# Splitting the rows of a triangular inverse over two copies, and moving copies of one recurrent branch from VectorE to ScalarE

## The chip, the cores and the metric

The kernel runs on one core of a Trainium2 chip. A core has TensorE (matrix products, into PSUM), VectorE (called DVE in the profile), ScalarE (ACT), GpSimd (POOL) and SyncE (SP, which here starts the weight loads). Each engine works through its own queue in order. The metric is the time of one execution on the device in microseconds; less is better.

## The reference

One transformer block, float32, 256 tokens of width 2048: half a SwiGLU feed-forward (hidden width 5632), a hybrid mixer, half a second feed-forward, each with a norm before and after. The mixer multiplies by `w_in`, sends 1024 columns each as r, k, v into a recurrent branch (16 heads of 64), 1024 into a pooling branch, and gates the two. The recurrent branch is, per head,

```python
def step(state, inp):
    r_t, w_t, k_t, v_t, a_t, b_t = inp
    sa = einsum('bhvk,bhk->bhv', state, a_t)
    state = state * w_t + sa[..., None] * b_t + v_t[..., None] * k_t
    y_t = einsum('bhvk,bhk->bhv', state, r_t)
```

with a = -kk and b = kk * a_h, where `kk` is k times `k_k`, normalised per head, and k itself is multiplied by `1 + (a - 1) * k_a`.

## The kernel before

Every large product is made of three float32r matmuls on a high and a low part of each operand (`mm3`, and the same three in `gemm_ch`). `load_w` brings a weight tile of 128 x 1024 in by SyncE's queue; ScalarE rounds it to wH (L101) and VectorE subtracts to get wL (L102). There are four buffers of the raw tile and five each of wH and wL. TensorE then runs 512-column matmuls (`gemm_tok`, L109 to L111) or 256-column ones (`gemm_ch`, L174 to L176).

The mixer runs in the order `a0 p a1 b0 b1 b2 b3`: recurrent branch for the first 512 channels, the four pooling windows (`pool_window`, L516 evacuates a product into zb; `pool_mix`, L547 and L548 write yb), the recurrent branch for the other 512, then the pooled projection. `rwkv` is the recurrent branch and is called twice ("half-branches" below). It turns the recurrence into chunks of 64 tokens:

- L584 to L649 work out the decay sums (lam, ilam by an exponential), kk (L609, normalised through pn and pk), k2 (L636, L638), and the per-head sums.
- L668 to L680 make a copy of v with neighbouring heads swapped, transpose it on TensorE (pV, L674) and copy it into EVs (ScalarE) and ODs (VectorE).
- L685 to L695 build the operands BK and AR. L706 multiplies them: eight PSUM tiles pA, each holding four chunks of one head's 64 x 64 products. ScalarE copies the first product into Xab (L710); VectorE masks the second into Xrb (L711) and the other half of the partitions back into AR (L713). pB transposes BK (L720, L724).
- The strictly triangular 64 x 64 matrix of each of the 16 (pair, chunk) groups per partition half must be inverted. Its two 32 x 32 diagonal blocks are inverted on VectorE. Four transposes (L733), one per 32 partitions, put the matrices on partitions: of each 32 partitions, 16 hold the 16 matrices and the other 16 hold a second copy of the same. Then 31 steps each make a product (L740, into pr) and add it (L742), over all rows found so far; both copies do the same work. Two transposes bring the inverse back (L746 to t11, L747 to td), L753 and L755 copy it into tt, and pM and pX (L761, L770) make the off-diagonal block.
- For each chunk, pU, pSa, pS and pY apply the inverse and carry the state; then a group norm and the output yH, yL.

All tiles of `rwkv` lie in fifteen registers `s.R[n]` of 128 x 1024 (in the profile they are all called R). PSUM has a pool of four tiles for the products above (mm, mc) and four for the small ones (pV, pA and so on). The program only states the work; the order of the instructions in each engine's queue is set when it is built, by a planner that simulates their costs, and weight conversions and most evacuations of `gemm_tok` and `gemm_ch` have raised priority.

Of the kernel before, what the change touches and what calls it, by code (L numbers as in the profile page):

```python
# [10 lines left out]
AF = mybir.ActivationFunctionType  # L11
ALU = mybir.AluOpType
AX = mybir.AxisListType
PSUM = bass.MemoryType.PSUM

P = 128
# [8 lines left out]
C = 64  # L25
# [19 lines left out]
class Block:  # L45
# [279 lines left out]
    def setup_mixer(s, prm):  # L325
        nc = s.nc
        s.col = {}

        def load_rows(rows, name):
            n = sum(r for _, r in rows)  # L330
            t = s.unit((P, 1024), F32, name)
            nc.gpsimd.memset(t[:, :P], 0.0)
            o = 0
            offs = []
            for nme, r in rows:
                offs.append((nme, o, r))
                if nme == "mu":
                    nc.sync.dma_start(out=t[o:o + 26, :P],
                                      in_=prm["mu"][:26 * P].rearrange("(k p) -> k p", p=P))
                    nc.sync.dma_start(out=t[o + 26:o + 27, :RCOLS - 26 * P],  # L340
                                      in_=prm["mu"][26 * P:].unsqueeze(0))
                    o += 27
                    continue
                nc.sync.dma_start(out=t[o:o + r, :P],
                                  in_=prm[nme].rearrange("(k p) -> k p", p=P))
                o += r
            ps = s.psum("pr")
            nc.tensor.transpose(ps[:, :P], t[:, :P], s.ident)
            ct = s.const([P, o], name)
            nc.vector.tensor_copy(ct, ps[:, :o])  # L350
            for nme, o, r in offs:
                s.col[nme] = ct[:, o:o + (27 if nme == "mu" else r)]

        load_rows(ROWS, "cols1")
        load_rows(ROWS2, "cols2")
        omu = s.const([P, 27], "omu")
        nc.vector.tensor_scalar(out=omu, in0=s.col["mu"], scalar1=-1.0, scalar2=1.0,
                                op0=ALU.mult, op1=ALU.add)
        s.col["omu"] = omu
        oka = s.const([P, 8], "oka")  # L360
        nc.vector.tensor_scalar(out=oka, in0=s.col["k_a"], scalar1=-1.0, scalar2=1.0,
                                op0=ALU.mult, op1=ALU.add)
        s.col["oka"] = oka
        m = s.mask = s.const([P, 2, C], "mask")
        nc.gpsimd.memset(m, 1.0)
        for h in range(2):
            for q, op in ((0, ALU.is_gt), (1, ALU.is_ge)):
                a = m[h * 64:h * 64 + 64, q]
                nc.gpsimd.affine_select(out=a, in_=a, compare_op=op, fill=0.0, base=0,
                                        pattern=[[1, C]], channel_multiplier=-1)  # L370
        s.bones = s.const([P, P], "bones")
        nc.gpsimd.memset(s.bones, 0.0)
        for h in range(2):
            nc.gpsimd.memset(s.bones[h * 64:h * 64 + 64, h * 64:h * 64 + 64], 1.0)
        s.zi = 0
        s.zb = [s.const([P, S + 16], f"zb{i}") for i in range(2)]
        for z in s.zb:
            nc.gpsimd.memset(z[:, :16], 0.0)
        s.rcp = s.const([P, 16], "rcp")
        for t in range(16):  # L380
            nc.gpsimd.memset(s.rcp[:, t:t + 1], 1.0 / (t + 1))
# [172 lines left out]
    def rwkv(s, hf, r, k, v, lz, prm, yH, yL):  # L554
        nc = s.nc
# [50 lines left out]
        kk = reg(3, 4, S)  # L606
        sq = reg(4, 4, S)
        for i in range(4):
            V.tensor_scalar(out=kk[:, i], in0=k[:, i], scalar1=col("k_k", i), scalar2=None,  # L609
                            op0=ALU.mult)  # L610
        A.activation(out=fl(sq), in_=fl(kk), func=AF.Square)
        ps = s.psum("pn")
        for i in range(4):
# [19 lines left out]

        k2 = reg(5, 4, S)
        for i in range(4):
            V.tensor_scalar(out=k2[:, i], in0=a[:, i], scalar1=col("k_a", i),  # L636
                            scalar2=col("oka", i), op0=ALU.mult, op1=ALU.add)
        V.tensor_tensor(out=fl(k2), in0=fl(k2), in1=fl(k), op=ALU.mult)  # L638


# [11 lines left out]
        BK = [reg(7, *t5), reg(8, *t5)]  # L652
        AR = [[reg(9, *t5), reg(10, *t5)], [reg(11, *t5), reg(12, *t5)]]
        EVs, ODs = reg(13, 4, NCH, C), reg(14, 4, NCH, C)
        Xab, Xrb = reg(4, 16, C), reg(5, 16, C)
        BKt = [reg(1, *t5), reg(2, *t5)]

        for q in range(2):
# [6 lines left out]
        vs = reg(10, 4, S)  # L665
        vp = lambda t: t.rearrange("p i (a b t) -> p (i a) b t", a=2, b=2)
        for b in range(2):
            V.tensor_copy(vp(vs)[:, :, b], vp(v)[:, :, 1 - b])  # L668
        for pr in range(2):
            pss = []  # L670
            for src in (v, vs):
                ps = s.psum("pV").rearrange("p (i c) -> p i c", i=4)
                for i in range(4):
                    T.transpose(ps[:, i], src[:, i, pr * P:pr * P + P], s.ident)  # L674
                pss.append(ps)
            for b in range(2):
                c = 2 * pr + b
                pe, po = pss[1 - b], pss[b]
                A.copy(EVs[O, :, c], pe[O, :, :64])
                V.tensor_copy(ODs[E, :, c], po[E, :, 64:])  # L680
        for q in range(2):
            i2 = slice(2 * q, 2 * q + 2)
            for h, R in ((0, E), (1, O)):
# [14 lines left out]
        for q in range(2):  # L698
            ar, bk = AR[q], BK[q]
            for i in range(2):  # L700
                g4 = slice(8 * q + 4 * i, 8 * q + 4 * i + 4)
                pAs = [s.psum("pA").rearrange("p (c j t) -> p c j t", c=NCH, j=2)
                       for _ in range(2)]
                for c in range(NCH):
                    for h, R in ((0, E), (1, O)):
                        T.matmul(pAs[h][:, c], bk[R, i, c], ar[h][R, i, c], start=True,  # L706
                                 stop=True)
                for h, R, RK in ((0, E, O), (1, O, E)):
                    ps = pAs[h]
                    A.copy(Xab[R, g4], ps[R, :, 0])  # L710
                    V.tensor_tensor(out=Xrb[R, g4], in0=ps[R, :, 1],  # L711
                                    in1=mb[R, :, 1].to_broadcast([64, NCH, C]), op=ALU.mult)
                    V.tensor_tensor(out=ar[h][RK, i], in0=ps[RK],  # L713
                                    in1=mb[RK].to_broadcast([64, NCH, 2, C]), op=ALU.mult)
            pBs = [s.psum("pB").rearrange("p (i c t) -> p i c t", i=2, c=NCH)
                   for _ in range(2)]
            for i in range(2):
                for c in range(NCH):
                    for h, R in ((0, E), (1, O)):
                        T.transpose(pBs[h][:, i, c],  # L720
                                    bk[R, i, c].rearrange("p j t -> p (j t)"),
                                    s.ident[R, R])
            for h in range(2):
                A.copy(BKt[q][:, :, :, h], pBs[h])  # L724
# [1 line left out]
        G.memset(ODs[O, :, 0], 0.0)  # L726


        wt, tw = reg(3, 32, 32), reg(0, 32, 32)
        for b in range(4):  # L730
            R = slice(b * 32, b * 32 + 32)
            o = (b % 2) * 32
            V.transpose(out=wt[R], in_=Xab[R, :, o:o + 32].rearrange("p g t -> p t g")  # L733
                        .unsqueeze(2).to_broadcast([32, 32, 2, 16]))
        G.memset(tw, 0.0)
        G.memset(s.R[0][:, 0:1024:33], 1.0)
        for kq in range(31):
            n, m = kq + 1, 31 - kq
            pr = s.rtmp("pr")[:, :n * m].rearrange("p (a b) -> p a b", a=n)
            V.tensor_tensor(out=pr, in0=wt[:, kq + 1:, kq].unsqueeze(1).to_broadcast([P, n, m]),  # L740
                            in1=tw[:, :n, kq:kq + 1].to_broadcast([P, n, m]), op=ALU.mult)
            V.tensor_tensor(out=tw[:, :n, kq + 1:], in0=tw[:, :n, kq + 1:], in1=pr,  # L742
                            op=ALU.add)
        tt, td, t11 = reg(7, 16, C), reg(8, 32, 32), reg(3, 32, 32)
        m1 = s.R[0][:, :512].rearrange("p (g t) -> p g t", g=16)
        V.transpose(out=t11, in_=tw)  # L746
        V.transpose(out=td, in_=tw.rearrange("p s t -> p t s"))  # L747
        for b in range(4):
            R = slice(b * 32, b * 32 + 32)
            o = (b % 2) * 32  # L750
            src = td[R, :, :16].rearrange("p t g -> p g t")
            if b < 2:
                A.copy(tt[R, :, o:o + 32], src)  # L753
            else:
                V.tensor_copy(tt[R, :, o:o + 32], src)  # L755
        for h in range(2):
            G.memset(tt[h * 64 + 32:h * 64 + 64, :, :32], 0.0)
        ps = s.psum("pM").rearrange("p (g t) -> p g t", g=16)
        for g in range(16):
            for h in range(2):  # L760
                T.matmul(ps[h * 64 + 32:h * 64 + 64, g],  # L761
                         Xab[h * 64:h * 64 + 32, g, 32:64],
                         t11[h * 64:h * 64 + 32, :, g], start=True, stop=True)
        A.copy(m1[32:64], ps[32:64])
        V.tensor_copy(m1[96:128], ps[96:128])
# [194 lines left out]
```

## Time and profile before

| | |
|---|---|
| median of 3 runs | 2156.44 us (2155.68 to 2157.66) |
| the profiled execution | 2156.19 us, its span 2154.4 us |
| TensorE busy | 2114.6 us, 98% of the span |
| VectorE busy | 1288.9 us, 60% |
| ScalarE busy | 1086.2 us, 50% |
| GpSimd busy | 78.2 us, 4% |
| mean granted TensorE clock | 0.992 |
| first half-branch, about | 856 to 1075 us |
| second half-branch, about | 1075 to 1280 us |

Busy time is the time in which an engine had an instruction in work. Matmuls overlap: a 512-column one is shown as 0.39 us long, but one starts every 0.226 us, so a busy TensorE may still run below its rate. A line such as "PE mc L174 <- DVE zb L516: 5.0, 1, 5.0" says that TensorE's matmul of line 174 waited 5.0 us in total, once, at most 5.0 us, for VectorE's write or read of zb in line 516. In the time order a row gives start, length, engine, line, operation, output and input with their shapes, and the count of instructions merged into it. The granted clock is TensorE's, as a share of full speed.

### The profile page before, as it was taken

How to read it: one execution, taken by the hardware profiler on the slowest of the kernel's cores; microseconds unless marked ns; L12 is line 12 of the kernel's file. 1: busy time of each engine (PE TensorE's matmuls, PEld its weight loads, DVE VectorE, ACT ScalarE, POOL GpSimd, SP SyncE). 2: the span in 40 equal slices, each digit the busy share in tenths (PEclk: the TensorE clock that was granted, in tenths of full speed). 3: DMA queues.
4: the chain of work that ended last, by engine and by line, in shares of the span. 5: the costliest groups of instructions: out<-in, count | busy, mean ns of one | idle time of the engine just before them, and what ended most of it. 6: DMA issues, size and time to landing. Idle time of an engine off the chain costs nothing.

```text
span 2154.4 us, 28711 instructions
## 1 busy us (share of the span) xinstructions
PE 2114.6 (98%) x11077; PEld 1774.9 (82%) x11077; DVE 1288.9 (60%) x1609; ACT 1086.2 (50%) x1516; POOL 78.2 (4%) x164
## 2 busy tenths in 40 slices
PE   8999999999999999889999999999999999999998
PEld 6888888888888799889788778878888888888886
DVE  5556555555444556997689656565556555654444
ACT  6565556555444554444454434455565556554442
POOL 1000000000000100101110110010000000000000
PEclk9999999999999999999999999999999999999999
DMA  7656666667666666255556666656667666676664
GB/s 234 195 177 207 195 195 186 198 205 242 195 195 192 194 173 182 84 157 164 147 153 179 178 223 193 192 179 202 194 177 213 193 191 184 206 252 192 193 193 136
DMA packets 223219, 406.06 MB, mean 188 GB/s; under 512 B 12991, under 2 KB 48969, under 8 KB 223081
## 3 DMA queue, kind: packets, MB, share of 16 engines
q1 hardware_dynamic: 216937, 383.11, 58.9%
q0 software_dynamic: 6144, 21.11, 2.7%
q8 instruction: 87, 1.43, 0.3%
q14 instruction: 51, 0.42, 0.1%
HBM read 395.78 MB, written 8.39 MB: 188 GB/s over the span
## 4 chain that ended last, share of the span: by engine, by line
PE 90%; DVE 6%; issue 2%; ACT 1%; DMA 1%; POOL 0%; DVEq 0%; POOLq 0%; SPq 0%; ACTq 0%
PE mm L111 27%; PE mm L110 27%; PE mm L109 27%; PE mc L174 2%; PE mc L175 2%; PE mc L176 2%; DVE wL L102 2%; DVE R L733 1%; DVE pr L740 1%; DMA w<-in_ffn_gate_dram 1%; ACT wH L101 0%; DVE R L742 0%; PE tr L206 0%; DVE R L713 0%; ACT junk L239 0%
## 5 line engine op out<-in xcount | busy, mean ns | idle before, releaser
L102 DVE TENSOR_TENSOR wL<-w,wH 128x1024 fp32r<-128x1024 f32 (+2 forms) x734 | 884.9, 1212 | 768.7 <-ACT wH L101 767.5
L101 ACT CAST wH<-w 128x1024 fp32r<-128x1024 f32 (+2 forms) x734 | 761.0, 1043 | 901.0 <-PE mm L111 708.8
L109 PE MATMUL mm<-wH,xH 128*128 128x512 f32 x2496 | 974.9, 391 | 6.7 <-ACT xH L212 6.7
L111 PE MATMUL mm<-wH,xL 128*128 128x512 f32 x2496 | 975.4, 391 | 5.2 <-DVE xL L213 5.2
L110 PE MATMUL mm<-wL,xH 128*128 128x512 f32 x2496 | 974.4, 391 | 0.5 <-DVE wL L102 0.4
L109 PEld LDWEIGHTS mm<-wH,xH 128*128 128x128 f32 x2496 | 470.3, 188 | 107.3 <-ACT xH L212 9.7
L111 PEld LDWEIGHTS mm<-wH,xL 128*128 128x128 f32 x2496 | 470.2, 188 | 104.4 <-DVE xL L213 6.8
L110 PEld LDWEIGHTS mm<-wL,xH 128*128 128x128 f32 x2496 | 470.2, 188 | 98.8 <-DVE wL L102 1.4
L174 PE MATMUL mc<-xH,wH 128*128 128x256 f32 (+1 forms) x560 | 160.3, 287 | 5.0 <-DVE zb L516 5.0
L175 PE MATMUL mc<-xH,wL 128*128 128x256 f32 x560 | 160.4, 287 | 0.0
L176 PE MATMUL mc<-xL,wH 128*128 128x256 f32 x560 | 159.5, 285 | 0.0
L232 ACT COPY x<-T 32x256 f32<-32x256 f32 x352 | 141.9, 403 | 3.9
L174 PEld LDWEIGHTS mc<-xH,wH 128*128 128x128 f32 (+1 forms) x560 | 107.0, 191 | 6.2 <-issue 5.4
L175 PEld LDWEIGHTS mc<-xH,wL 128*128 128x128 f32 x560 | 107.1, 191 | 0.6
L176 PEld LDWEIGHTS mc<-xL,wH 128*128 128x128 f32 x560 | 107.1, 191 | 0.4
L251 ACT ACTIVATE sg<-mm,rs 128x512 f32<-128x512 f32 x44 | 30.2, 690 | 21.3 <-PE mm L111 21.3
L252 DVE SCALAR_TENSOR_TENSOR sg<-mm,rs,sg 128x512 f32<-128x512 f32 x44 | 31.6, 751 | 13.2 <-ACT sg L251 13.2
L283 POOL DMA_DIRECT2D gb<-in_ln_ffn_post_dram x4 | 2.2, 562 | 926.7 <-DVE xL L236 893.5
L239 ACT ACTIVATE junk<-mm 128x512 bf16<-128x512 f32 x24 | 14.3, 595 | 34.5 <-PE mm L111 34.5
L286 DVE TENSOR_TENSOR fg<-mm,gb 128x512 f32<-128x512 f32 x24 | 16.5, 691 | 24.5 <-ACT junk L239 24.5
L257 DVE SCALAR_TENSOR_TENSOR sg<-mm,rs,sg 128x512 f32<-128x512 f32 x44 | 30.9, 744 | 0.0
L222 DVE STREAM_TRANSPOSE T<-sg 128x512 f32<-128x512 f32 x44 | 30.9, 702 | 0.0
(220 smaller groups left out, 1030.2 us busy)
## 6 DMA issues: line engine op xcount, KB each, us to landing
w<-in_ffn_up_dram SPq DMA_DIRECT2D x176, 512.0 KB
w<-in_ffn_down_dram SPq DMA_DIRECT2D x176, 512.0 KB
w<-in_ffn_gate_dram SPq DMA_DIRECT2D x174, 512.0 KB
w<-in_w_in_dram SPq DMA_DIRECT2D x128, 512.0 KB
w<-in_w_out_dram SPq DMA_DIRECT2D x32, 512.0 KB
w<-in_w_proj_b_dram SPq DMA_DIRECT2D x16, 512.0 KB
w<-in_w_proj_a_dram SPq DMA_DIRECT2D x16, 512.0 KB
hsp<-fg POOLq DMA_DIRECT2D x16, 256.0 KB, 5.1
```

The source lines that it names most:

```text
L101: nc.scalar.copy(vH, v)
L102: nc.vector.tensor_tensor(out=vL, in0=v, in1=vH.bitcast(F32), op=ALU.subtract)
L109: nc.tensor.matmul(ps, aH, bH, start=start, stop=False)
L110: nc.tensor.matmul(ps, aH, bL, start=False, stop=False)
L111: nc.tensor.matmul(ps, aL, bH, start=False, stop=stop)
L174: s.nc.tensor.matmul(o, h_, xH, start=k == 0, stop=False)
L175: s.nc.tensor.matmul(o, l_, xH, start=False, stop=False)
L176: s.nc.tensor.matmul(o, h_, xL, start=False, stop=k == KT - 1)
L222: s.nc.vector.transpose(out=T1[:, h * 512:h * 512 + 512], in_=src)
L232: nc.scalar.copy(dst[q * 32:q * 32 + 32, :, :, i], src[i * 32:i * 32 + 32, :, :, q])
L252: nc.vector.scalar_tensor_tensor(out=sg, in0=ps, scalar=rs[h], in1=sg, op0=ALU.mult, op1=ALU.mult)
L257: nc.vector.scalar_tensor_tensor(out=sig[h], in0=ps, scalar=rs[h], in1=sig[h], op0=ALU.mult, op1=ALU.mult)
```

## The change

In the recurrence, the two copies of each matrix now share the rows: copy d (0 or 1) holds rows d, d+2, d+4 and so on. So step kq covers kq // 2 + 1 rows instead of kq + 1, and tw is half as large. The ones on its diagonal are set by two ScalarE copies from a new constant `dup` (128 x 2, made once from the identity) in place of a GpSimd fill. The way back is two transposes of 128 x 512, the second reading the first's result, in place of two of 128 x 1024.

The diagonal blocks are no longer transposed out of Xab in four pieces. ScalarE copies them out of each pA tile in two pieces of 32 partitions into Xd, laid out with the 16 matrices adjacent, and the off-diagonal block in a third piece into Xo; Xd and Xo share the register that Xab had. One transpose of 128 x 1024, which reads Xd twice, makes wt.

Four kinds of VectorE instructions with one tensor input move to ScalarE: kk's product, k2's scale and bias, the swapped copy of v, and the ODs copies. So do the two copies into tt that VectorE made.

```diff
--- before.py
+++ after.py
@@ -368,6 +368,9 @@
                 a = m[h * 64:h * 64 + 64, q]
                 nc.gpsimd.affine_select(out=a, in_=a, compare_op=op, fill=0.0, base=0,
                                         pattern=[[1, C]], channel_multiplier=-1)
+        s.dup = s.const([P, 2], "dup")
+        nc.vector.tensor_reduce(out=s.dup, in_=s.ident.rearrange("p (b d g) -> p d b g", b=4, d=2),
+                                axis=AX.XY, op=ALU.add)
         s.bones = s.const([P, P], "bones")
         nc.gpsimd.memset(s.bones, 0.0)
         for h in range(2):
@@ -606,8 +609,7 @@
         kk = reg(3, 4, S)
         sq = reg(4, 4, S)
         for i in range(4):
-            V.tensor_scalar(out=kk[:, i], in0=k[:, i], scalar1=col("k_k", i), scalar2=None,
-                            op0=ALU.mult)
+            A.activation(out=kk[:, i], in_=k[:, i], func=AF.Copy, scale=col("k_k", i))
         A.activation(out=fl(sq), in_=fl(kk), func=AF.Square)
         ps = s.psum("pn")
         for i in range(4):
@@ -633,8 +635,8 @@
 
         k2 = reg(5, 4, S)
         for i in range(4):
-            V.tensor_scalar(out=k2[:, i], in0=a[:, i], scalar1=col("k_a", i),
-                            scalar2=col("oka", i), op0=ALU.mult, op1=ALU.add)
+            A.activation(out=k2[:, i], in_=a[:, i], func=AF.Identity, scale=col("k_a", i),
+                         bias=col("oka", i))
         V.tensor_tensor(out=fl(k2), in0=fl(k2), in1=fl(k), op=ALU.mult)
 
 
@@ -652,7 +654,9 @@
         BK = [reg(7, *t5), reg(8, *t5)]
         AR = [[reg(9, *t5), reg(10, *t5)], [reg(11, *t5), reg(12, *t5)]]
         EVs, ODs = reg(13, 4, NCH, C), reg(14, 4, NCH, C)
-        Xab, Xrb = reg(4, 16, C), reg(5, 16, C)
+        Xrb = reg(5, 16, C)
+        Xd = s.R[4][:, :512].rearrange("p (t g) -> p t g", g=16)
+        Xo = s.R[4][:, 512:].rearrange("p (g t) -> p g t", g=16)
         BKt = [reg(1, *t5), reg(2, *t5)]
 
         for q in range(2):
@@ -665,7 +669,7 @@
         vs = reg(10, 4, S)
         vp = lambda t: t.rearrange("p i (a b t) -> p (i a) b t", a=2, b=2)
         for b in range(2):
-            V.tensor_copy(vp(vs)[:, :, b], vp(v)[:, :, 1 - b])
+            A.copy(vp(vs)[:, :, b], vp(v)[:, :, 1 - b])
         for pr in range(2):
             pss = []
             for src in (v, vs):
@@ -677,7 +681,7 @@
                 c = 2 * pr + b
                 pe, po = pss[1 - b], pss[b]
                 A.copy(EVs[O, :, c], pe[O, :, :64])
-                V.tensor_copy(ODs[E, :, c], po[E, :, 64:])
+                A.copy(ODs[E, :, c], po[E, :, 64:])
         for q in range(2):
             i2 = slice(2 * q, 2 * q + 2)
             for h, R in ((0, E), (1, O)):
@@ -707,7 +711,11 @@
                                  stop=True)
                 for h, R, RK in ((0, E, O), (1, O, E)):
                     ps = pAs[h]
-                    A.copy(Xab[R, g4], ps[R, :, 0])
+                    for o in (0, 32):
+                        A.copy(Xd[h * 64 + o:h * 64 + o + 32, :, g4]
+                               .rearrange("p t g -> p g t"),
+                               ps[h * 64 + o:h * 64 + o + 32, :, 0, o:o + 32])
+                    A.copy(Xo[h * 64:h * 64 + 32, g4], ps[h * 64:h * 64 + 32, :, 0, 32:])
                     V.tensor_tensor(out=Xrb[R, g4], in0=ps[R, :, 1],
                                     in1=mb[R, :, 1].to_broadcast([64, NCH, C]), op=ALU.mult)
                     V.tensor_tensor(out=ar[h][RK, i], in0=ps[RK],
@@ -726,40 +734,37 @@
         G.memset(ODs[O, :, 0], 0.0)
 
 
-        wt, tw = reg(3, 32, 32), reg(0, 32, 32)
-        for b in range(4):
-            R = slice(b * 32, b * 32 + 32)
-            o = (b % 2) * 32
-            V.transpose(out=wt[R], in_=Xab[R, :, o:o + 32].rearrange("p g t -> p t g")
-                        .unsqueeze(2).to_broadcast([32, 32, 2, 16]))
+
+        wt = reg(3, 32, 32)
+        tw = s.R[0][:, :512].rearrange("p (s t) -> p s t", s=16)
+        V.transpose(out=wt, in_=Xd.unsqueeze(2).to_broadcast([P, 32, 2, 16]))
         G.memset(tw, 0.0)
-        G.memset(s.R[0][:, 0:1024:33], 1.0)
+        for d in range(2):
+            A.copy(s.R[0][:, d:512:34], s.dup[:, d:d + 1].to_broadcast([P, 16]))
         for kq in range(31):
-            n, m = kq + 1, 31 - kq
+            n, m = kq // 2 + 1, 31 - kq
             pr = s.rtmp("pr")[:, :n * m].rearrange("p (a b) -> p a b", a=n)
             V.tensor_tensor(out=pr, in0=wt[:, kq + 1:, kq].unsqueeze(1).to_broadcast([P, n, m]),
                             in1=tw[:, :n, kq:kq + 1].to_broadcast([P, n, m]), op=ALU.mult)
             V.tensor_tensor(out=tw[:, :n, kq + 1:], in0=tw[:, :n, kq + 1:], in1=pr,
                             op=ALU.add)
-        tt, td, t11 = reg(7, 16, C), reg(8, 32, 32), reg(3, 32, 32)
-        m1 = s.R[0][:, :512].rearrange("p (g t) -> p g t", g=16)
+        tt = reg(7, 16, C)
+        t11 = s.R[3][:, :512].rearrange("p (s g) -> p s g", g=16)
+        td = s.R[3][:, 512:].rearrange("p (g t) -> p g t", g=16)
+        m1 = s.R[0][:, 512:].rearrange("p (g t) -> p g t", g=16)
         V.transpose(out=t11, in_=tw)
-        V.transpose(out=td, in_=tw.rearrange("p s t -> p t s"))
-        for b in range(4):
+        V.transpose(out=td, in_=t11.rearrange("p s g -> p g s"))
+        for b in (1, 3, 0, 2):
             R = slice(b * 32, b * 32 + 32)
             o = (b % 2) * 32
-            src = td[R, :, :16].rearrange("p t g -> p g t")
-            if b < 2:
-                A.copy(tt[R, :, o:o + 32], src)
-            else:
-                V.tensor_copy(tt[R, :, o:o + 32], src)
+            A.copy(tt[R, :, o:o + 32], td[R])
         for h in range(2):
             G.memset(tt[h * 64 + 32:h * 64 + 64, :, :32], 0.0)
         ps = s.psum("pM").rearrange("p (g t) -> p g t", g=16)
         for g in range(16):
             for h in range(2):
                 T.matmul(ps[h * 64 + 32:h * 64 + 64, g],
-                         Xab[h * 64:h * 64 + 32, g, 32:64],
+                         Xo[h * 64:h * 64 + 32, g],
                          t11[h * 64:h * 64 + 32, :, g], start=True, stop=True)
         A.copy(m1[32:64], ps[32:64])
         V.tensor_copy(m1[96:128], ps[96:128])
```

## The prediction

> **What bounds the kernel now.** I read the shares of the engines first, then the waits of TensorE, then a table of stretches around the waits, then VectorE's queue there. The span is one TensorE stream with few holes in it:
>
> ```profile
> span 2154.4 us, 28711 instructions
> PE 2114.6 (98%) x11077; PEld 1774.9 (82%) x11077; DVE 1288.9 (60%) x1609; ACT 1086.2 (50%) x1516; POOL 78.2 (4%) x164
> ```
>
> TensorE's matrix work is not touched, so a change of VectorE and ScalarE work counts only where TensorE waits for it. Between 850 and 1300 us, the stretch in which the recurrent branch runs twice, TensorE waits this often (us in total, times, longest):
>
> ```profile
> PE mc L174 <- DVE zb L516: 5.0, 1, 5.0
> PE pA L706 <- DVE R L695: 3.8, 1, 3.8
> PE mc L174 <- DVE yb L548: 1.1, 1, 1.1
> PE pM L761 <- DVE R L746: 0.9, 1, 0.9
> PE pA L706 <- DVE R L713: 0.8, 1, 0.8
> PE pB L720 <- DVE R L713: 0.6, 1, 0.6
> PE pA L706 <- ACT R L724: 0.4, 1, 0.4
> PE mm L110 <- DVE wL L102: 0.4, 1, 0.4
> ```
>
> With 0.3 for pk that is 13.3 us, nearly all for VectorE. All but the pM and wL waits lie in the first half-branch, where VectorE has no free time (columns: stretch, its length, busy time and count of PE, PEld, DVE, ACT, POOL, granted clock, DMA share, GB/s):
>
> ```profile
> 880.00:900.00 20.00, 16.20 (x121) 15.47 (x119) 19.69 (x37) 6.37 (x13) 1.10 (x2) 0.90 0.36 94
> 900.00:920.00 20.00, 18.19 (x157) 17.01 (x157) 19.02 (x34) 7.97 (x15) 1.03 (x2) 0.93 0.14 48
> 920.00:940.00 20.00, 14.98 (x113) 14.81 (x113) 19.04 (x46) 6.27 (x9) 0.00 (x0) 0.91 0.56 158
> 940.00:960.00 20.00, 18.85 (x156) 18.62 (x156) 19.97 (x48) 9.13 (x13) 0.00 (x0) 1.00 0.63 181
> ```
>
> The granted clock adds to it. In the time order of TensorE, 256-column matmuls start every 0.12 us, but after the 3.8 us hole 11 of them start every 0.213 and 24 of pA every 0.157 instead of 0.10, and after the 5.0 us hole 15 start every 0.213: 11 x 0.093 + 24 x 0.055 + 15 x 0.094 = 3.7 us. In the second half seven 512-column matmuls after pM start every 0.427 instead of 0.226: 1.4 us. So at most 12.0 + 3.7 in the first half and 1.3 + 1.4 in the second can be won: 18.4 us. The longest hole is made by what stands ahead of an evacuation in VectorE's queue:
>
> ```profile
> 911.27 4.08 DVE L733 STREAM_TRANSPOSE R<-R 32x1024 f32<-32x1024 f32 x2
> 916.50 4.08 DVE L733 STREAM_TRANSPOSE R<-R 32x1024 f32<-32x1024 f32 x2
> 926.37 0.42 DVE L516 TENSOR_TENSOR zb<-mc,rsb 128x256 f32<-128x256 f32 x1
> 926.94 0.55 PE L174 MATMUL mc<-xH,wH 128*128 128x256 f32 x1 [5.02 <-DVE zb L516]
> ```
>
> **The change part by part, per half-branch. VectorE loses:**
> - the kk product, 4 x 0.344 (L609) = 1.4; k2's first step, 4 x 0.405 (L636) = 1.6; the swapped copy of v, 2 x 0.42 (L668) = 0.8; the ODs copies, 4 x 0.411 (L680) = 1.6;
> - four transposes of 2.03 (L733) = 8.1, for one of 128x1024. It costs 1.24 if it runs like L746 (contiguous input), 2.03 if like L733; its input runs over 16 adjacent elements, so I take 1.6: 6.5 saved;
> - the row recurrence. Its 31 steps keep their count, but cover 2856 instead of 5456 elements per partition. The rows by shape give 0.20 (31 elements) to 0.65 (256) for L740 and 0.20 to 0.43 for L742; interpolated over all steps 25.5 falls to 17.6: 7.9 saved;
> - the two transposes after it: L746 1.24 to 0.70 (L222, 128x512), L747 1.95 to about 1.05 (its fixed part near 0.15, the rest halved): 1.4 saved;
> - two copies of 0.67 into tt (L755): 1.3.
>
> That is 22.5 us less. Up to 960 some 12 of it fall due in the first half: L680 1.6, L733 6.5, and about 4 of the 13.4 us that the first 16 steps take (7.8 and 5.6).
>
> **ScalarE gains** kk and k2 at 0.50 each as L390 (128x256, a pointer scale), 8 x 0.50 = 4.0; v's swap 2 x 0.62 (L858) = 1.2; ODs 4 x 0.368 (L679) = 1.5; the ones of tw 2 x 0.19 (L447) = 0.4. The 8 copies of Xab (0.367 each, 2.9) become 24 copies of 128 elements: the 8 contiguous ones at 0.273 (L415), the 16 strided ones between 0.273 and 0.42 (L753 reads with a stride: 1.094 for 512 elements, so 0.19 + 128 x 0.0018): 6.6 to 8.9. The tt copies stay near 2.3. Sum 11 to 13 us more, against 50 us in which ScalarE is idle of the 80 between 880 and 960. The weight casts behind these copies are covered as long as that idle time lasts; without the cover each us late is a us of TensorE.
>
> **POOL** fills half as much of tw and no ones; it waited 17 us for its input, nothing follows. Its first copy into the ea area now overlaps m1 and waits for pX: that is where tt is completed, which pSa needs anyway, so nothing. The dup reduction in the set-up is one VectorE instruction of about 0.3 (L826 took 0.415 for twice the size), in a stretch where TensorE waits for xL: 0 to 0.3, I take 0.3. No DMA is issued anew, SP's queue is passed by nothing, and weight loads start earlier where wL frees their buffers earlier.
>
> **What reaches TensorE.**
> 1. The zb hole, 5.0 + 1.4 of slow clock. VectorE's queue ahead of L516 shortens by 6.5, more than the hole: all 6.4 gone (0 if the planner puts other work there).
> 2. The yb hole, 1.1: the recurrence steps ahead are halved: gone (0 to 1.1).
> 3. The pA hole, 3.8 + 2.3. Three of the L680 copies go (1.2), L636 too (1.4); but k2 now runs on ScalarE between the sigmoid (ends 861.5) and the exponential that VectorE's L646 was waiting for (1.19 idle), which delays lam by about 1. Net 1.7 earlier: 1.7 of the hole, and half of the slow clock, 1.1. Bounds 0 and 6.1. After the 1.1 us hole no slow clock is seen, after 3.8 it is; but pM's 0.87 was followed by the seven slow matmuls, which is why I take half. The Trainium skill (TensorE: Matmul & The Clock Gate, Part 1: The HAM clock gate) has the clock halve only after an idle window of about 3.4 us; by that a hole of 2.1 would cost no clock, all 2.3 would return and the sum would be 2144.6. The 0.87 us wait here does not fit it well.
> 4. The pA/pB holes of 1.8. L711 waited for L710's end on the same tile (0.67 us at 908), so a tile is read by ScalarE, then by VectorE: 0.37 + 0.42 + 0.69 = 1.5 now, 1.1 + 1.1 = 2.2 later at the strided price. Over 8 tiles that is up to 5.9 more. VectorE reads one tile while ScalarE reads the next, and four buffers are there, so I take 1.0 longer; bounds -1.8 and +5.9.
> 5. Second half: the wL and pM holes and the clock, 2.7; pM's input still comes through one transposition, so I take half, 1.4.
>
> Gains 6.4 + 1.1 + 1.7 + 1.1 - 1.0 + 1.4 - 0.3 = 10.4. The profiled execution took 2156.19 (span 2154.4 and 1.8 around it), 0.25 under the median of the three: 2156.2 - 10.4 = 2145.8, say 2146.
>
> **The rivals.**
> *Slower:* ScalarE becomes the bound of the pA stage. The place is L710: three copies per tile before VectorE may read it. For: the wait of L711 on L710, and the two rows with a stride. Against: ScalarE's idle there, 5.3 and 2.9 us at a time. Strictly serial it costs 5.9 in each half on TensorE's path, with 1.4 of slow clock after each, 14.6; less holes 1 and 2 (7.5) the kernel is 7.1 slower: 2163. To be 4.3 slower, 11.8 must come back on TensorE's path: 9.0 of stage beside 2.8 of clock, which needs most of the strided price in both halves and no overlap. The Trainium skill (PSUM — Partial Sum Buffer, PSUM bank collisions raise a hardware error) asks that two engines' reads of one bank and quadrant be kept apart, reads against reads included; by that rule this chain cannot be shortened by overlapping on one tile, and the waits of L711 agree.
>
> *Hidden anyway, or given back:* holes 1 and 2 go, the first half's pA stage takes the full 5.9: 1.6 won, 2154.6. For: the order in each queue is the planner's, TensorE runs in order, and a hole can move to another line; second-half VectorE is also over 90% busy and TensorE lost only 1.3 there. Against: VectorE's saving is on the very instructions ahead of L516.
>
> *All of it:* every hole and slow clock goes, 18.4: 2137.8. Against: pA still needs the whole chain up to L695.
>
> That the change does not do what it says would show as unchanged element counts in L740; the slices `:n` with n = kq // 2 + 1 fix them, so I give it nothing.
>
> **How the numbers follow.** Three runs spread over 2 us, so 0.2% (4.3 us) is about what a measurement can tell from no change. Forecast 0.57 (2139 to 2151.9), all of it 0.05, hidden or given back 0.25 (2151.9 to 2160.5), ScalarE as the bound 0.13. So faster 0.62, same 0.25, slower 0.13. The range leaves out all of it (0.05), the slower rival (0.13) and the upper end of the hidden one (0.02): 2139 to 2157. The forecast's own range is 2139 to 2152.
>
> **What would show it.** L740 with shapes up to 128x136 and a sum near 10 in place of 15 us per half; one L733 of 1.2 to 2.0; no wait of mc for zb, none for yb; a pA wait of 1 to 3 us; granted clock 1.00 in 920 to 940; VectorE below 90% busy from 900 to 1000 (96% before). Wrong would be: ScalarE's L710 group above 9 us per half with TensorE waiting for pA's tiles, weight casts waiting behind it, or a new wait of over 3 us in place of zb's.

## The result and the profile after

The changed kernel takes 2139.22 us (median of four runs, 2135.83 to 2140.30), the kernel before 2156.98 beside it (2155.68 to 2157.66): a ratio of 0.9918, with a 95% interval of 0.9902 to 0.9933. The profiled execution took 2139.63 us, so it is 16.6 us shorter than the one that the prediction's sum was made against (2156.19). The prediction said 10.4 less and 2146.

The shares of the engines, after:

```profile
span 2137.9 us, 28747 instructions
PE 2109.0 (99%) x11077; PEld 1771.1 (83%) x11077; DVE 1246.9 (58%) x1572; ACT 1106.9 (52%) x1584; POOL 75.9 (4%) x162
```

VectorE works 42.0 us less and ScalarE 20.7 more, 21.0 and 10.4 per half-branch. TensorE's waits between 850 and 1300 us, after (total, times, longest); this is the whole list:

```profile
PE mc L174 <- DVE yb L551: 0.9, 1, 0.9
PE mc L174 <- DVE zb L519: 0.2, 1, 0.2
```

Of 13.3 us of waits 1.1 are left, and the slow clock behind them is gone. The stretches of the first half-branch, after (same columns as before):

```profile
880.00:900.00 20.00, 19.76 (x158) 19.06 (x157) 19.73 (x40) 10.32 (x21) 1.02 (x2) 1.00 0.51 161
900.00:920.00 20.00, 20.00 (x193) 18.89 (x192) 19.67 (x44) 14.56 (x34) 2.16 (x4) 1.00 0.34 105
920.00:940.00 20.00, 19.12 (x158) 18.86 (x158) 20.00 (x61) 9.36 (x15) 0.00 (x0) 1.00 0.66 204
940.00:960.00 20.00, 20.00 (x169) 20.00 (x169) 18.98 (x41) 10.21 (x15) 0.00 (x0) 1.00 0.66 201
```

The granted clock is 1.00 throughout, and TensorE is never idle for long. But VectorE, which has less to do, is as busy as it was: 78.4 of these 80 us. It does its work earlier, not at a lower share. What differs is which work stands where. VectorE's queue in time order, after (four rows of it; others stand between them):

```profile
890.96 0.76 DVE L519 TENSOR_TENSOR zb<-mc,rsb 128x256 f32<-128x256 f32 x2
891.63 2.80 DVE L689 TENSOR_TENSOR R<-R,R 64x512 f32<-64x512 f32 x4
896.99 0.69 DVE L699 TENSOR_TENSOR R<-zr,R 64x512 f32<-64x512 f32 x1
913.54 1.24 DVE L740 STREAM_TRANSPOSE R<-R 128x1024 f32<-128x1024 f32 x1
```

and the kernel before at the same place:

```profile
889.79 2.80 DVE L685 TENSOR_TENSOR R<-R,R 64x512 f32<-64x512 f32 x4
894.89 0.69 DVE L695 TENSOR_TENSOR R<-zr,R 64x512 f32<-64x512 f32 x1
896.05 0.76 DVE L516 TENSOR_TENSOR zb<-mc,rsb 128x256 f32<-128x256 f32 x2
```

L695, for whose end 24 pA matmuls waited 3.8 us, is now L699, and it ends later: 897.68 against 895.58. Yet nobody waits for it. The pooling evacuation zb now comes ahead of the operand builds (L689), so TensorE has pooling products to do meanwhile. Its time order before, and after (in the second, rows are left out between the two):

```profile
890.76 1.16 PE L706 MATMUL pA<-R,R 64*128 64x128 f32 x8
895.72 3.77 PE L706 MATMUL pA<-R,R 64*128 64x128 f32 x24 [3.80 <-DVE R L695]
```

```profile
894.74 1.16 PE L710 MATMUL pA<-R,R 64*128 64x128 f32 x8
900.33 1.71 PE L710 MATMUL pA<-R,R 64*128 64x128 f32 x21
```

Before, the first 8 and the next 24 pA matmuls stand back to back in the queue. After, 36 matmuls of the pooling product stand between them, about 4.5 us of work (the trace shows 21 of the 24 in one row and three more behind it). I call these two the old and the new order. They are kinds and not single queues: the new one has 36 pooling matmuls at that place in the change, e2, e7, e8 and e10, 39 in e1, e5 and e9, and 23 in e12, and kernels of one kind can differ further on.

Where the time was won can be counted: the moment at which TensorE has done the same number of 256- and 512-column matmuls in both kernels. After is 0.9 us late when the branch begins, 15.2 early at 970 us, 17.2 early at the end of the second half-branch, 16.6 at the end. So the first half-branch gives 16.0, the second 2.0, and 1.5 are lost outside (the kernels of the experiments lie between 1.8 us early and 1.4 late when the branch begins, with and without the set-up of `dup`, so I read nothing into that).

The sizes of the operations, after, in the groups of both half-branches (busy us, mean ns):

```profile
L747 DVE TENSOR_TENSOR pr<-R,R 128x126 f32<-128x126 f32 (+22 forms) x62 | 19.9, 321 | 1.3
L749 DVE TENSOR_TENSOR R<-R,pr 128x126 f32<-128x126 f32 (+22 forms) x62 | 15.5, 251 | 1.2
L740 DVE STREAM_TRANSPOSE R<-R 128x1024 f32<-128x1024 f32 x2 | 2.5, 1242 | 0.0
L715 ACT COPY R<-pA 32x128 f32<-32x128 f32 x32 | 11.9, 372 | 7.0 <-PE pA L710 6.5
L718 ACT COPY R<-pA 32x128 f32<-32x128 f32 x16 | 4.1, 256 | 0.2
L638 ACT ACTIVATE R<-R,oka,cols 128x256 f32<-128x256 f32 x8 | 4.4, 631 | 0.0
```

The recurrence costs 17.7 per half instead of 25.5, and the gather costs ScalarE 8.0 per half instead of 2.9 and saves VectorE 6.9 of transposes.

### The profile page after: what moved, and what is told of

Same layout as the page of the kernel before. It is cut to its first block, busy times and chain, and to the rows that moved or that the text cites. A ratio compares the mean times of both kernels' runs of the same rounds, so it can differ in the third digit from the quotient of the medians.

```text
span 2137.9 us, 28747 instructions
## 1 busy us (share of the span) xinstructions
PE 2109.0 (99%) x11077; PEld 1771.1 (83%) x11077; DVE 1246.9 (58%) x1572; ACT 1106.9 (52%) x1584; POOL 75.9 (4%) x162
## 4 chain that ended last, share of the span: by engine, by line
PE 95%; DVE 2%; ACT 1%; issue 1%; DMA 1%; DVEq 0%; POOLq 0%; POOL 0%; SPq 0%; ACTq 0%
PE mm L110 28%; PE mm L111 28%; PE mm L109 28%; PE mc L174 3%; PE mc L175 3%; PE mc L176 3%; DVE wL L102 1%; DMA w<-in_ffn_gate_dram 1%; PE tr L206 0%; ACT junk L239 0%; ACT wH L101 0%; PE pU L787 0%; DVE fg L307 0%; PE pSa L798 0%; PE pA L710 0%
## 5 line engine op out<-in xcount | busy, mean ns | idle before, releaser
L251 ACT ACTIVATE sg<-mm,rs 128x512 f32<-128x512 f32 x44 | 30.1, 690 | 20.7 <-PE mm L111 20.7
```

## The experiments

The table puts all of them together. "Less" is VectorE's busy time below that of before, per half-branch, from the shares of the engines. "Order" is the place of the pooling products in TensorE's queue. "Transposes" is how many stand where L733 stood. "Us faster" is (1 - ratio) times the median of before in the same comparison. The last two columns are the gain in the first and in the second half-branch, by the count of matmuls in the profiled execution; what lies outside the branch is not in them.

| kernel | less | order | transposes | ratio, 95% interval | us faster | first half | second half |
|---|---|---|---|---|---|---|---|
| the change | 21.0 | new | 1 | 0.9918 (0.9902 to 0.9933) | 17.7 | 16.0 | 2.0 |
| e5 split, gather, k2 | 17.6 | new | 1 | 0.9923 (0.9908 to 0.9937) | 16.6 | 15.0 | 3.2 |
| e8 gather, four moves | 11.6 | new | 1 | 0.9925 (0.9908 to 0.9942) | 16.2 | 14.9 | 2.9 |
| e9 gather, k2 | 8.2 | new | 1 | 0.9939 (0.9927 to 0.9952) | 13.1 | 14.4 | -1.6 |
| e7 the change, 6 transposes | 15.1 | new | 6 | 0.9949 (0.9934 to 0.9963) | 11.0 | 7.3 | 2.0 |
| e10 split, four moves | 14.8 | new | 4 | 0.9962 (0.9949 to 0.9976) | 8.2 | 6.8 | 2.0 |
| e2 four moves | 4.6 | new | 4 | 0.9975 (0.9966 to 0.9985) | 5.4 | 5.6 | -0.7 |
| e1 k2 alone | 1.6 | new | 4 | 0.9972 (0.9961 to 0.9982) | 6.0 | 4.0 | 2.6 |
| e12 more work | 0.0 | new | 4 | 0.9977 (0.9968 to 0.9986) | 5.0 | 2.9 | 1.8 |
| e6 the change without k2 | 19.0 | old | 1 | 0.9937 (0.9923 to 0.9952) | 13.6 | 11.5 | 0.3 |
| e3 split, gather | 16.2 | old | 1 | 0.9967 (0.9953 to 0.9981) | 7.1 | 5.8 | 0.3 |
| e4 gather alone | 6.3 | old | 1 | 0.9986 (0.9977 to 0.9996) | 3.0 | 2.6 | 1.0 |
| e11 split alone | 9.7 | old | 4 | 0.9985 (0.9976 to 0.9994) | 3.2 | 1.5 | 2.3 |

Two theories stood at first: *load* (the holes close because VectorE has less to do ahead of them) and *order* (the pA hole closes because the queues are ordered anew). Later two more: *amount* (the gain follows the work taken off VectorE) and *place* (it follows what is taken off ahead of a hole).

**e1: only k2's step on ScalarE.** The edit, against the kernel before:

```diff
         for i in range(4):
-            V.tensor_scalar(out=k2[:, i], in0=a[:, i], scalar1=col("k_a", i),
-                            scalar2=col("oka", i), op0=ALU.mult, op1=ALU.add)
+            A.activation(out=k2[:, i], in_=a[:, i], func=AF.Identity, scale=col("k_a", i),
+                         bias=col("oka", i))
```

> The kernel before with one part of the change alone: k2's scale and bias on ScalarE (1.6 us per half-branch off VectorE, nothing else). The planner's TensorE queue differs from the kernel before around pA: 4 instructions groups of pA, then 39 products of the pooling stage, then the other pA, where before all 16 stand together. Load theory (what counts is VectorE work taken off ahead of a hole): the zb hole of 5.0 us stays, the pA hole shrinks from 3.8 to 2.4 or so; 1 to 2.5 us faster than before. Order theory (what counts is that other products stand between pA's in TensorE's queue, so that it does not wait while VectorE builds the operands): no pA wait on L695 at all, its slow clock and the small pA/pB waits gone too, zb hole as before; 5 to 8 us faster, though VectorE is relieved of only 1.6 us.

6.0 us faster, as by the order theory, for 1.6 us of VectorE work. In the profiled execution 4.0 of it come in the first half-branch and 2.6 in the second, where the pM wait is gone. Its first half-branch: VectorE's queue, TensorE's waits, and the stretch of the longest:

```profile
897.94 0.69 DVE L695 TENSOR_TENSOR R<-zr,R 64x512 f32<-64x512 f32 x1
```

```profile
PE mc L174 <- ACT mxT L535: 8.0, 1, 8.0
PE mc L174 <- DVE zb L516: 0.7, 1, 0.7
PE mc L174 <- DVE yb L548: 0.4, 1, 0.4
```

```profile
920.00:940.00 20.00, 11.61 (x73) 10.79 (x73) 19.79 (x46) 4.71 (x7) 0.00 (x0) 0.78 0.49 144
```

L695 ends 3.0 us later than before, and no pA matmul waits for it. The hole did not vanish, though: VectorE's backlog reaches the four transposes (915.4 to 925.9 here), and the pooling work queued behind them makes a hole of 8.0 where zb's was 5.0: TensorE waits there for mxT, the pooled tile that its next products read.

**e2: the four moves to ScalarE, without split and gather.**

```diff
-            V.tensor_scalar(out=kk[:, i], ...
+            A.activation(out=kk[:, i], ...
...
-            V.tensor_scalar(out=k2[:, i], ...
+            A.activation(out=k2[:, i], ...
...
-            V.tensor_copy(vp(vs)[:, :, b], vp(v)[:, :, 1 - b])
+            A.copy(vp(vs)[:, :, b], vp(v)[:, :, 1 - b])
...
-                V.tensor_copy(ODs[E, :, c], po[E, :, 64:])
+                A.copy(ODs[E, :, c], po[E, :, 64:])
```

> The kernel before with all four moves of single-input steps to ScalarE (kk, k2, swapped v, ODs; 5.4 us per half-branch off VectorE), without the split rows and without the single transpose. Load theory: pA hole shorter by 2 to 3 us, zb hole still near 5; 3 to 5 us faster. Order theory: pA and pA/pB waits and their slow clock gone (7.9 us), zb hole stays unless products moved behind it cover it; 7 to 10 us faster.

5.4 us, nearer to the load theory's number, but the pA wait is gone here too; what is left of the evacuation holes is zb 3.7, mxT 1.4 and 1.3. So neither theory had the time right: the new order came, and its gain went into the same hole as in e1.

**e3 and e4: split and gather without the moves, and the gather alone.** e3 takes the four moves of e2 back out of the changed kernel. e4 has, of the change, only this:

```diff
-                    A.copy(Xab[R, g4], ps[R, :, 0])
+                    for o in (0, 32):
+                        A.copy(Xd[h * 64 + o:h * 64 + o + 32, :, g4]
+                               .rearrange("p t g -> p g t"),
+                               ps[h * 64 + o:h * 64 + o + 32, :, 0, o:o + 32])
+                    A.copy(Xo[h * 64:h * 64 + 32, g4], ps[h * 64:h * 64 + 32, :, 0, 32:])
...
-        for b in range(4):
...
-            V.transpose(out=wt[R], in_=Xab[R, :, o:o + 32].rearrange("p g t -> p t g")
-                        .unsqueeze(2).to_broadcast([32, 32, 2, 16]))
+        V.transpose(out=wt, in_=Xd.unsqueeze(2).to_broadcast([P, 32, 2, 16]))
```

> The changed kernel with the four moves undone: kk, k2, swapped v and ODs stay on VectorE; rows split and diagonal blocks gathered as in the change (17 us per half-branch off VectorE). TensorE's queue around pA is as in the kernel before. Load theory: most of the gain, 12 to 14 us faster, the pA hole shorter since VectorE is freer. Order theory: the pA wait on L695 stays near 3.8 and the clock falls after it; only the zb and yb holes and the second half go, 7 to 10 us faster.

> The kernel before with the diagonal blocks gathered by ScalarE and one transpose of 128 x 1024 in place of four (6.9 us per half-branch off VectorE); rows not split, no moves. Both theories: the zb hole (5.0 and 1.4 of slow clock) goes, the pA hole stays at 3.8 or more, since the work ahead of it is the same; 5 to 7 us faster. If ScalarE's third copy per tile costs TensorE something, pA/pB waits above the 1.8 us of before and a gain below 5.

7.1 us for e3, as by the order theory; 3.0 for e4, less than the 5 to 7 expected. The longest waits of e4:

```profile
PE pA L708 <- DVE R L697: 3.8, 1, 3.8
PE mc L174 <- DVE zb L516: 2.8, 2, 2.0
```

e3 has the same 3.8 for pA, and 1.3 for zb. With the old order the pA hole stays whole; what e3 takes off VectorE, 16.2 us per half, stands behind it. And in e4 the zb hole closes only by half, although the transposes ahead of it fell from 8.1 to 1.25: nine steps of the recurrence and three weight conversions now stand ahead of zb. The prediction had named this as its bound ("0 if the planner puts other work there").

**e5: split, gather and k2; e8: gather and the four moves.** e5 is the changed kernel with kk, the swapped v and ODs back on VectorE; e8 is the changed kernel with the recurrence and what follows it as before:

```diff
-            n, m = kq // 2 + 1, 31 - kq
+            n, m = kq + 1, 31 - kq
```

> Row split and gather as in the change, and of the four moves only k2's (18.6 us per half-branch off VectorE). TensorE's queue around pA is that of the changed kernel: products between the first pA's and the rest. Theory of two conditions (the order that k2's move brings, and the relief that split and gather bring; each alone only moves the hole): no pA wait, zb and yb under 2 us, 15 to 18 us faster, that is the sum of the single runs (6.6 and 6.2 by TensorE's progress) and a few us more. Load theory (relief alone): 18.6 of 22.5, so 12 to 14 us faster.

> The changed kernel without the row split: gather and the four moves as in the change, the recurrence over all rows as before (12 us per half-branch off VectorE). TensorE's queue around pA as in the changed kernel. Two conditions: no pA wait, holes of 2 to 4 us in the recurrence (yb, mxT, zb) between 925 and 960, 11 to 15 us faster. If the split is worth nothing there: 16 to 18.

Both are as fast as the change within the intervals, and the holes of 2 to 4 us that were expected in e8 did not come (the longest is 1.2). So beside the gather and k2 the other three moves are worth nothing that can be measured (3.4 us of VectorE work per half), and beside the gather and the moves the row split is not either (9.4 us). Alone, the split gives 3.2 (e11).

**e6: the changed kernel with k2 back on VectorE** (e1's edit reversed).

> The changed kernel with k2's scale and bias alone put back on VectorE (1.6 us per half-branch). All 16 first pA's stand together again in TensorE's queue. Two conditions: a pA wait on L695's counterpart of 2.5 to 4 us and slow clock return, 8 to 12 us faster than the kernel before, so 6 to 9 of the 17 lost for 1.6 us of work. Load theory: 15 to 17 us faster, little lost.

13.6 us, between the two numbers, with an interval that touches both, so the trace has to decide (in the first half-branch it wins 11.5, the change 16.0). In its built order 32 pA matmuls stand back to back again, and the old wait is back, shorter, with its slow clock:

```profile
895.26 3.75 PE L710 MATMUL pA<-R,R 64*128 64x128 f32 x24 [2.53 <-DVE R L699]
```

```profile
880.00:900.00 20.00, 17.47 (x131) 16.74 (x130) 19.71 (x40) 10.87 (x26) 0.53 (x1) 0.86 0.42 118
```

This separates the prediction's step 3 into its parts: without k2 and the new order the other moves shorten the pA hole by 1.3 us (the 1.7 forecast had k2's part in it) and leave the clock slow behind it; the rest came with k2. It also limits the order theory. In the old order the three other moves are worth 6.5 us (e3 against e6); beside k2 they are worth nothing that can be measured. They and k2 can stand in for each other in part. But e3 and e6 do not have one queue either: TensorE's differ from 887 us on, so how much of the 6.5 is work and how much is order is not shown.

**e7: the changed kernel with the one transposition made six times** (of the same data).

```diff
-        V.transpose(out=wt, in_=Xd.unsqueeze(2).to_broadcast([P, 32, 2, 16]))
+        for _ in range(6):
+            V.transpose(out=wt, in_=Xd.unsqueeze(2).to_broadcast([P, 32, 2, 16]))
```

> The changed kernel with the single transpose L740 made six times over into the same register (5 x 1.24 = 6.2 us per half-branch of VectorE work added, where the kernel before had its four transposes of 8.1); the result is the same. TensorE's queue around pA stays that of the changed kernel. Two conditions: a hole of 3 to 6 us behind the transposes (on zb, yb or mxT), 8 to 13 us faster than the kernel before. Order alone: no hole, 15 us or more.

11.0 us, with a hole as expected, and TensorE's queue is that of the change up to this hole:

```profile
PE mc L174 <- ACT mxT L538: 5.8, 1, 5.8
```

So 6.2 us of VectorE work at that place cost 6.7 us (8.7 in the first half-branch by the count of matmuls; the granted clock is 0.74 in 920 to 940). The 9.4 us that the split takes off, behind that place, are worth 1.5 or nothing (e8). The place decides.

**e9: the gather and k2 alone; e10: everything but the gather; e11: the split alone.** These set amount against place: e9 takes 8.2 us off VectorE per half, e10 nearly twice that.

> The smallest pair that should do it: the gather with one transpose, and k2's scale and bias on ScalarE; rows not split, kk, swapped v and ODs on VectorE as before (8.5 us per half-branch off VectorE, of the 22.5 of the change). Theory of place (relief counts only where it stands ahead of a hole, and the order must be the one that k2's move brings): 15 to 18 us faster, no different from the whole change. Theory of amount (the hole time goes with the VectorE work taken off): 5 to 10 us faster.

> The counterpart: row split and all four moves, but four transposes of 2.03 us out of Xab as before (16 us per half-branch off VectorE, twice as much as in the smallest pair). Place: the products pushed behind the transposes meet a hole of 4 to 8 us there, as with k2 alone; 6 to 10 us faster. Amount: 12 to 16 us faster.

> The row split alone, with the smaller way back (10.6 us per half-branch off VectorE); nothing gathered, nothing moved. TensorE's queue around pA as in the kernel before. Place: pA and zb holes as before, the yb hole and part of the second half's 2.7 gone; 1 to 4 us faster. Amount: 6 to 9 us faster.

e10 and e11 gave 8.2 and 3.2, as by place. e9 with half the work of e10 gave 13.1, more than by amount and less than by place. By the count of matmuls it had all but 1.6 of the first half-branch's gain; in the second it lost 1.6, where the change won 2.0, by a wait at its end:

```profile
PE mm L109 <- ACT yH L860: 3.8, 1, 3.8
```

With all rows in the 31 recurrence steps there, the branch's output yH is ready at 1277.1 us, and TensorE, which is earlier than in the kernel before, has to wait for it. In the change yH is ready at 1246.7. That is what the split is good for beside the gather and k2: it gives back the wait that the earlier arrival makes. In e8, which differs from e9 by the other three moves, it is ready at 1271.6, and there is no wait.

Four of these kernels make the plainest test of place. The change, e8 (no split), e10 (no gather) and e2 (neither) have the same TensorE queue up to 914 us, past the last pA. In the first half-branch the gather wins 9.3 us with the split (from 6.8 to 16.0) and 9.3 without it (from 5.6 to 14.9). The split wins 1.2 with the gather and 1.2 without it, though it takes 9 to 10 us off VectorE, and the gather 6 to 7.

**e12: the kernel before with more work for VectorE.** Its copies are read by nothing.

```diff
+        for _ in range(4):
+            V.tensor_copy(s.rtmp("dm"), fl(kk)[:, :256])
         V.tensor_tensor(...
```

> The kernel before with four copies of 128 x 256 added on VectorE ahead of L649 in each half-branch, whose results nothing reads: nothing is taken off VectorE, and about 4 x 0.4 = 1.6 us per half are put on. In the built order the queue of TensorE changes as it did with k2 alone on ScalarE: 4 products of pA, then 23 matmuls of the pooling product, then the next 12 of pA, in place of 16 of pA in one stretch. Order theory (the pA hole goes because VectorE's queue has zb ahead of the operand builds, not because VectorE has less to do): no wait of pA for L697 (L695 of before) of over 1 us and no slow clock behind it, a hole of 7 to 11 us moved to the transposes of L733 or the next evacuation after them, and the time 0 to 5 us under the kernel before. Load theory (the pA hole is short or gone where VectorE has less to do ahead of it): the pA wait grows from 3.8 to 4 to 6 us, the other holes stay, and the time is 1 to 4 us over the kernel before.

It is 5.0 us faster. The eight copies of both halves take 1.9 us in their group, less than the 1.6 per half expected. Nothing is taken away, yet VectorE's total is 1288.9, as before, so such a total can be off by about 1 us per half. The new order came with the copies (23 pooling matmuls between the first 8 and the next 24 of pA). TensorE's waits around pA, and the one behind the transposes:

```profile
890.98 1.13 PE L708 MATMUL pA<-R,R 64*128 64x128 f32 x8 [1.73 <-DVE R L687]
893.91 0.58 PE L174 MATMUL mc<-xH,wH 128*128 128x256 f32 x1 [1.80 <-DVE zb L516]
899.02 1.71 PE L708 MATMUL pA<-R,R 64*128 64x128 f32 x21
922.85 0.58 PE L174 MATMUL mc<-xH,wH 128*128 128x256 f32 x1 [6.33 <-DVE zb L516]
```

Nothing waits for L697 (L695 of before), as the order theory had it, and the load theory's slower kernel did not come. But its hole at the evacuation behind the transposes is 6.3, not the 7 to 11 expected, and the pA place gains little: 1.73 for the first operands and 1.80 for zb, with 23 matmuls at half the clock (23 x 0.093 = 2.1), are 5.6 us in place of 6.1. Order alone is not what wins there. In e1 the same place costs 0.7, with 2.6 less for VectorE to do per half (1.6 for k2 and half of 1.9). So each theory has half. With the old order 2.8 us of moves shorten the pA hole by 1.3 (e3 to e6); with the new one 2.6 us go with 4.9 less there (e12 to e1). The queues of both pairs differ in their detail too, so these two figures are not the price of VectorE's work alone.

Nor are all of the 5.0 won at the holes of the first half-branch: 2.9 are, by the count of matmuls, and 1.8 come in the second, where there is no pM wait. In the profiled execution, the fastest of the eleven, another 2.9 lie outside the branch, where this kernel's program is that of before.

## Why the prediction was right or wrong

The sign was right, and at the zb hole the mechanism too (VectorE's queue ahead of TensorE's evacuations). The size was not: 10.4 forecast, 16.6 measured, since at pA something else was at work (step 3). The measured 2139.22 lies 0.2 us inside the forecast's own range of 2139 to 2152, and that is luck: the sum said 2146. It is nearer to the rival "all of it" (2137.8), to which I had given 5 in 100.

*Step 1, the zb hole, 6.4: right.* 0.2 is left and the clock in 920 to 940 is 1.00. The reason given, a saving of 6.5 that exceeds the hole, was too simple. Alone, the gather leaves 2.8 of it (e4), the moves without the gather 3.7 (e2), and the closing of the pA hole alone makes it larger (8.0 in e1): a hole that closes upstream brings TensorE sooner to the next one. Both had to be there. e7 shows the size: 6.2 us more at that place, and a hole of 5.8 is back.

*Step 2, the yb hole, 1.1: wrong, and small.* 0.9 is left.

*Step 3, the pA hole, 1.7 + 1.1 of 6.1: this is the step that failed.* All 6.1 came back, 3.3 more than I took. I had argued that VectorE would reach L695 1.7 us earlier. It reached it 2.1 later (0.9 of that because the branch begins later). The order of the queues, which I had held fixed, changed: e6 (k2 back, 2.5 us of hole) gives 1.3 for the work taken off, and e1 shows the hole gone for 1.6 us of work. The argument against "all of it", that pA still needs the whole chain up to L695, was true and did not matter: in the new order TensorE has other products to run meanwhile. The hole had also cost more than the 6.1 counted. Of the rows shown, 24 pA take 3.77 us behind the wait, and 21 take 1.71 in the change; 24 would take about 2.0 at that pace, so the slow clock lost an estimated 1.8 on them, not 1.3. This is part of why the first half-branch won 16.0 and has 1.1 of waits left, where I had set 15.7 as the most it could win; the rest of that difference stays open. Why the planner orders so with k2 moved, or with four copies added that nothing reads, stays open. The Trainium skill (TensorE: Matmul & The Clock Gate, Part 1: The HAM clock gate) would have had no clock lost behind a hole of 2.1. Of the runs, e4's 2.0 at 924.2 is followed by a granted clock of 1.00, which agrees; e6's 2.53 and e12's 1.73 and 1.80 within 3 us of each other are followed by matmuls every 0.213 us, though each is shorter than the idle window of about 3.4 us that the page gives.

*Step 4, the pA and pB holes, 1.0 longer: wrong.* The 1.8 went, so the term was off by 2.8. The price was right: the 24 copies take 8.0 us per half (forecast 6.6 to 8.9), with 372 ns for the strided ones, inside 273 to 420. But the copies do not lie on TensorE's path. In the new order pA comes in parts of 8, 24, 24 and 8 matmuls, with 36, 23 and 9 pooling matmuls between them, and the evacuations have that time. In two kernels of the old order the gather did make these holes longer, 2.3 in e3 and e4 for 1.8 before; in e6, of the old order too, they are 1.1.

*Step 5, the second half, 1.4 of 2.7: a little low, and near by luck.* 2.0 by the count of matmuls. There is no pM wait any more. But the transposition need not be the reason: e12, which takes nothing off VectorE, wins 1.8 there and e1 2.6, both without a pM wait. What moves that wait stays open.

*The set-up, 0.3 lost:* 0.9 ahead of the branch and 0.6 behind it, 1.5 in all. The 0.9 is within the scatter named above.

The sum by steps: 16.0 in the first half-branch for 9.3 (6.4 + 1.1 + 1.7 + 1.1 - 1.0), 2.0 for 1.4, -1.5 for -0.3. The costs of the parts held: recurrence 17.7 for 17.6, the second transposition after it 1.08 for 1.05, VectorE 21.0 for 22.5, ScalarE 10.4 for 11 to 13. Of those off, the transposition of 128x1024 took 1.24, not 1.6, and k2 0.63, not 0.50.

*The rivals.* ScalarE did not become a bound: it is idle for 35.6 of the 80 us. "Hidden or given back" did not come with the whole change, but in e1, e2 and e10 it did: there the closed pA hole comes back at the transposes. Of the marks named, the recurrence's sums, the single transposition, the granted clock and VectorE below 90% in 900 to 1000 (87.7%) were met; a pA wait of 1 to 3 was not, and the yb wait did not go.

## What to carry to other kernels

Where a planner sets the order of the queues, an edit does two things, it takes work away and it orders anew, and the second can be the larger one: 1.6 us moved gave 6.0 (4.0 of it in the first half-branch), and work added gave 5.0 (2.9 of it there). Such orders can change from one small edit to the next, as the 39, 36 and 23 matmuls here show. So list the built order of the queues of both kernels around each hole before the sum is made; it costs no run. And take work off in front of the next hole too: a saturated engine hands a closed hole on to the next wait on it, so k2 (6.0) and the gather (3.0) are worth 13.1 together.

## What the runs showed of the hardware

A transposition that reads runs of 16 adjacent elements costs what a contiguous one costs: L740 took 1.24 us for 128x1024, as L746 of before, whereas L733 took 2.03 for 32 partitions of the same length, with stride. A ScalarE copy of 32x128 out of PSUM took 372 ns when it wrote with a stride of 16 elements, and 256 when it wrote adjacent ones. ScalarE's pass over 256 elements took 499 ns with one pointer operand (L612, function Copy) and 631 with two (L638, function Identity; 608 in e1). The Trainium skill (ScalarE: Activation LUTs, What ACT_TABLE_LOAD costs) gives about 93 ns for each pointer operand; the 109 to 132 here are somewhat more, and the two passes differ in their function as well.
